# Reordering the projections of a retention head, and moving its value transposes, in a two-layer streaming trunk on one Trainium2 core

## The chip, the cores and the metric

The kernel runs on one core of a Trainium2 chip. The metric is the device time of one execution in microseconds (us), the median of three runs; one execution was profiled besides, and all rows below come from it.

## What is computed

Two layers over 528 tokens (16 learned ones ahead of 512) and 1024 channels. Each layer normalises its input, projects it into 14 x 1024 channels, runs a short convolution branch and a retention branch with four heads, gates both, projects the sum and adds it to the residual:

```python
for l in range(DEPTH):
    xn = _rmsnorm(h, pre_norm_g[l])
    proj = xn @ w_in[l] + b_in[l]
    c_h, c_b, c_c, c_z, r_q, r_k, r_v, r_z, g_a, g_b = jnp.split(proj, split_at, axis=-1)
    y_a = _short_conv_branch(c_h, c_b, c_c, c_z, conv_w[l], conv_b[l], w_conv_out[l])
    y_b = _retention_branch(r_q, r_k, r_v, r_z, ret_gn_g[l], w_ret_out[l])
    y = jax.nn.sigmoid(g_a) * y_a + jax.nn.sigmoid(g_b) * y_b
    h = h + _rmsnorm(y @ w_o[l], post_norm_g[l])
```

In the retention branch a head has 256 query and key channels, 512 value channels and 512 gate channels. Queries and keys are rotated by position, scores of query and key are weighted with a decay and multiplied with the values; the result is normalised per head and token, multiplied with silu of the gate channels, and projected back with w_ret_out.

## The kernel before, in words

Channels lie on the partitions and tokens along the free axis. All products are made with fp32r operands in two parts (hi and lo), three matmuls for one: hi x hi, hi x lo, lo x hi. ScalarE makes the hi part (a cast, L142) and VectorE the lo part (a subtraction, L143), for weights as for activations.

The projections run in `Group`s (L284): one group makes 256 output channels for all tokens, by a block scheme with seven products (`mul`, L275) of 12 matmuls each. Six of them run in the group itself; the seventh, with the call that hands over the result (`end`, L358), runs behind the first two products of the next job (`close`). Each product is evicted by ScalarE (`put`, L322, rows of L325, and L335) into SBUF; a group uses two PSUM tiles `pb` and `pc` and the shared `pa`. `RetOut` (L521) multiplies a quarter of the previous head's finished output with w_ret_out: two results of 24 matmuls each (L244) into a two-bank PSUM tile `pp`, of which there are two; VectorE adds the result to YB (L540), for head 0 ScalarE copies it (L538).

Between these jobs stands the work on whole heads. It is put into the stream by `later(delay, fn)` (L127): after `delay` more ticks, and a tick is one product of a group, or half of one result of `RetOut`: 12 matmuls in both cases (6 where 512 tokens go in one piece). What is called there for a head:

- `rope` (L395): the rotation of keys or queries, two steps of three VectorE operations (L403 to L405) and a split each; called when the group of the keys or queries ends (`k_done`, `q_done`).
- `scores` (L412), 8, 10 and 12 ticks behind the end of the queries.
- `vtrans` (L441): PE transposes values by token block (L447) into `pp`; per block ScalarE evicts twice (L454 with a read of its accumulator, L455; once L459) and VectorE once (L460). Called 3, 6 and 9 ticks behind the end of the second group of values (`v_done`, L844), where also two sets of tiles are taken and ScalarE copies the last 64 tokens twice (`twice`).
- behind the end of the second group of gates (`z_done`, L855): `attend` (L463) at 1, 3, 5 and 7 ticks, each with evictions L492, L493 and the sum of squares L496; the sum over partitions and its power (`rstd_token`, L366: PE L370, VectorE L374, GpSimd L375) at 10; its spreading over the partitions (`spread`, L378: PE L384, ScalarE L387) at 13; and the normalisation of the four result tiles (`finish`: VectorE L514, then a split) at 14 to 17. These four tiles are what `RetOut` of this head reads, in the stream of the next head.

For heads 1 to 3 the order of jobs is keys, queries, first values, two `RetOut`, second values, two `RetOut`, gates, gates (L883 and below); head 3's `RetOut`s stand among groups of the convolution branch. Head 0 has another order, written out at the start of each layer, and its own delays (16 or 12 ticks for the transposes).

The framework records these calls in program order and then orders the instructions of each engine by priority and by when its own model holds an operand for ready; so instructions of neighbouring jobs change places. Every engine then runs its list strictly in that order. Tiles of SBUF with the tag `r` come from one pool of 26.

Of the kernel before, what the change touches and what calls it, by code (L numbers as in the profile page):

```python
# [25 lines left out]
DK = 256  # L26
DV = 512
# [6 lines left out]
R_Q = 4 * D  # L34
R_K = R_Q + H * DK
R_V = R_K + H * DK
# [20 lines left out]
def trunk(ctx: ExitStack, tc: tile.TileContext, xT, w_in, binT, w_co, w_ro, w_o, gpre, gpost,  # L57
# [19 lines left out]
    def rslot(w=T):  # L77
        return gr.tile([P, w], F32R, tag="r", name=nm("r"))

    def fslot(w=T, dt=F32):  # L80
        return gr.tile([P, w], dt, tag="r", name=nm("f"))
# [45 lines left out]
    def later(delay, fn):  # L127
        now[1] += 1
        heappush(queue, (now[0] + delay, now[1], fn))
# [260 lines left out]
    def twice(dst, src):  # L390

        nc.scalar.copy(dst.rearrange("p (a b) -> p a b", a=2),
                       src[:, T - CHUNK:T].unsqueeze(1).to_broadcast([P, 2, CHUNK]))
# [47 lines left out]
    def vtrans(vt, v8, V, js):  # L441

        pp = pslot()
        for b, j in enumerate(js):
            k0, kn, _ = JT[j]
            for v in range(4):
                nc.tensor.transpose(pp[0:kn, b, v * P:(v + 1) * P], vt[v][:, k0:k0 + kn] if j < 4 else v8[:, v, :], ident)  # L447
        for b, j in enumerate(js):
            kn = JT[j][1]
            pv = pp[0:kn, b, :]  # L450
            s = sm.tile([P, 1], F32, tag="vs", name=nm("vs"))[0:kn]
            hi, lo = V[j]
            with tc.high_priority():
                nc.scalar.activation(hi[0:kn], pv, AF.Copy, scale=-1.0 / DV, accum_out=s)  # L454
                nc.scalar.activation(hi[0:kn], pv, AF.Identity, bias=s)  # L455
                r0 = 0
                if j == len(JT) - 1:
                    r0 = CHUNK
                    nc.scalar.activation(lo[0:r0], pv[0:r0], AF.Identity, bias=s[0:r0])  # L459
                nc.vector.scalar_tensor_tensor(lo[r0:kn], pv[r0:kn], s[r0:kn], hi[r0:kn].bitcast(F32),  # L460
                                               op0=ALU.add, op1=ALU.subtract)
# [334 lines left out]
    for l in range(DEPTH):  # L796
# [7 lines left out]
        hd = heads(0)  # L804
# [12 lines left out]
        def add(job, *args, todo=todo):  # L817
            todo.append((job, args))
            return job

        def k_done(ts, hd):
            a, b, hd["k"] = rope(ts, 0)

            def k8():
                hd["k8"] = rslot(512).rearrange("p (n c) -> p n c", n=4)
                for n in range(4):
                    twice(hd["k8"][:, n, :], hd["k"][n // 2][n % 2].bitcast(F32))
            later(0, a)
            later(2, b)
            later(3, k8)  # L830
# [13 lines left out]
        def v_done(ts, hd, d=3):  # L844
            hd["vt"] = hd.get("vt", []) + list(ts)
            if len(hd["vt"]) == 4:
                vt = hd["vt"]
                v8 = fslot(512).rearrange("p (v c) -> p v c", v=4)
                for v in range(4):
                    twice(v8[:, v, :], vt[v])  # L850
                hd["V"] = V = [(rslot(512), rslot(512)) for _ in JT]
                for n, js in enumerate(((0, 1), (2, 3), (4,))):
                    later(d + 3 * n, lambda js=js: vtrans(vt, v8, V, js))

        def z_done(ts, hd, h, l, yr, silu=(1,)):  # L855
            cs = slice(QCOLS[l].t0, T)
            for n in silu:
                nc.scalar.activation(ts[n][:, cs], ts[n][:, cs], AF.Silu)
            hd["zt"] = hd.get("zt", []) + list(ts)
            if len(hd["zt"]) < 4:  # L860
                return

            def start():
                hd["sums"] = fslot()
                hd["n"] = normed(l, hd["zt"], hd["sums"], yr)
            later(0, start)
            for v in range(4):
                later(1 + 2 * v, lambda v=v: attend(l, h, *hd["S"], hd["V"], v, hd["zt"][v], hd["sums"]))
            later(10, lambda: hd["n"][0]())
            later(13, lambda: hd["n"][1]())  # L870
            for v in range(4):
                later(14 + v, lambda v=v: hd["n"][2](v))

        hd["done"] = (k_done, q_done, v_done, z_done)
        yrs = jb["yrs"] = [[] for _ in range(H)]
# [6 lines left out]
        add_conv(0)  # L882
        for h in range(1, H):  # L883
            d = {}
            add(Group(l, R_K + h * DK, I_ALL[l], lambda ts, d=d: k_done(ts, d)))
            add(Group(l, R_Q + h * DK, I_Q[l], lambda ts, d=d, h=h, l=l: q_done(ts, d, h, l)))
            add(Group(l, R_V + h * DV, I_ALL[l], lambda ts, d=d: v_done(ts, d)))
            for q in (0, 1):
                add(RetOut(l, h - 1, q), yrs[h - 1])
            add(Group(l, R_V + h * DV + 256, I_ALL[l], lambda ts, d=d: v_done(ts, d)))  # L890
            for q in (2, 3):
                add(RetOut(l, h - 1, q), yrs[h - 1])
            for b in range(2):
                add(Group(l, R_Z + h * DV + b * 256, I_Q[l],
                          lambda ts, d=d, h=h, l=l, yr=yrs[h]: z_done(ts, d, h, l, yr), AF.Silu))
# [364 lines left out]
```

## Time and profile before

| | us |
|---|---|
| median of 3 runs | 1603.13 |
| lowest and highest run | 1600.23, 1605.2 |
| the profiled execution | 1600.25 |
| its span, first to last instruction | 1598.4 |
| PE (matmul) busy | 1553.9 |
| VectorE (DVE) busy | 1168.9 |
| ScalarE (ACT) busy | 910.2 |

How to read it: PE matmuls overlap, so their busy time is longer than the distance between their starts; a wait is idle time of an engine just ahead of an instruction, put down to what came last. Times in a row count from the span's start. A window row gives the PE's granted clock as a share of full speed (2.4 GHz): 1.00 is that level, 0.50 the other, 1.2 GHz.

### The profile page before, as it was taken

The page shows a single profiled execution, that of the slowest core. Times are in us where ns is not written, and L with a number is a line of the kernel's source. Part 1 is how long each engine was busy: PE and PEld are TensorE (multiplying, and loading weights), DVE is VectorE, ACT ScalarE, POOL GpSimd, SP SyncE. Part 2 cuts the span into 40 slices and gives each one's busy share as a digit, 9 for nine tenths or more (in the row PEclk, how much of TensorE's full clock was granted, in tenths as well). Part 3 has the DMA queues.
Part 4 walks back from the last instruction along what each step waited for, and adds up shares of the span by engine and source line. Part 5 has one row for each costly group of instructions (what it writes and reads, how often), then busy time and mean ns, then how long its engine had stood idle before and what let it go on. Part 6 is the DMA issues. An engine that isn't in the chain of part 4 may idle for free.

```text
span 1598.4 us, 29227 instructions
## 1 busy us (share of the span) xinstructions
PE 1553.9 (97%) x11762; PEld 1494.1 (93%) x11762; DVE 1168.9 (73%) x1702; ACT 910.2 (57%) x1763; POOL 28.9 (2%) x23
## 2 busy tenths in 40 slices
PE   9999999899999999999999999999999999999998
PEld 9989999898999999999999998998998999999986
DVE  6996966776776788866376889678777777997542
ACT  6675565464565466655345666655654655676531
POOL 0000000001000000000000000000000000000000
PEclk9999999999999999999999999999999999999999
DMA  7132332232222243335321223222322223334421
GB/s 263 67 113 73 106 107 89 83 108 97 89 103 87 91 141 128 133 123 180 119 101 53 100 94 113 103 103 95 111 93 80 101 98 119 132 126 145 142 98 53
DMA packets 86039, 174.37 MB, mean 109 GB/s; under 512 B 11280, under 2 KB 15888, under 8 KB 85904
## 3 DMA queue, kind: packets, MB, share of 16 engines
q1 hardware_dynamic: 85760, 172.50, 31.2%
q8 instruction: 92, 1.51, 0.4%
q14 instruction: 43, 0.35, 0.1%
q10 hardware_dynamic: 144, 0.01, 0.0%
HBM read 168.21 MB, written 4.26 MB: 108 GB/s over the span
## 4 chain that ended last, share of the span: by engine, by line
PE 79%; DVE 10%; ACT 5%; issue 3%; DMA 3%; POOL 1%; SPq 0%; DVEq 0%; POOLq 0%; ACTq 0%
PE pb L279 25%; PE pp L244 15%; PE pc L279 13%; PE pp L648 7%; PE pa L279 6%; PE pp L481 4%; PE pp L1122 3%; PE pb L648 3%; DVE wlo L143 2%; PE pp L422 2%; DMA raw<-in_w_in 2%; ACT whi L142 2%; DVE r L143 1%; PE pp L384 1%; PE pp L447 1%
## 5 line engine op out<-in xcount | busy, mean ns | idle before, releaser
L143 DVE TENSOR_TENSOR wlo<-raw,whi 128x1024 fp32r<-128x1024 f32 (+2 forms) x358 | 392.7, 1107 | 120.4 <-ACT whi L142 117.5
L142 ACT CAST whi<-raw 128x1024 fp32r<-128x1024 f32 (+2 forms) x358 | 339.4, 959 | 227.8 <-PE pp L244 63.7
L279 PE MATMUL pb<-Xh,whi 128*128 128x264 f32 (+2 forms) x1008 | 287.7, 285 | 2.2 <-ACT pa L335 1.2
L279 PE MATMUL pb<-Xl,whi 128*128 128x264 f32 (+2 forms) x1008 | 285.0, 283 | 0.0
L279 PE MATMUL pb<-Xh,wlo 128*128 128x264 f32 (+2 forms) x1008 | 284.7, 283 | 0.1
L244 PE MATMUL pp<-r,whi 128*128 128x264 f32 (+1 forms) x1152 | 251.2, 325 | 5.6 <-ACT r L142 4.8
L279 PE MATMUL pc<-Xh,whi 128*128 128x264 f32 (+2 forms) x672 | 194.4, 289 | 8.1 <-ACT f L325 7.8
L244 PEld LDWEIGHTS pp<-r,whi 128*128 128x128 f32 x1152 | 176.3, 188 | 23.7 <-ACT r L142 5.9
L279 PEld LDWEIGHTS pb<-Xh,whi 128*128 128x128 f32 x1008 | 189.6, 188 | 4.4 <-ACT pa L335 1.6
L279 PE MATMUL pc<-Xl,whi 128*128 128x264 f32 (+2 forms) x672 | 192.0, 286 | 0.0
L279 PE MATMUL pc<-Xh,wlo 128*128 128x264 f32 (+2 forms) x672 | 191.5, 285 | 0.0
L279 PEld LDWEIGHTS pb<-Xl,whi 128*128 128x128 f32 x1008 | 189.6, 188 | 0.6
L279 PEld LDWEIGHTS pb<-Xh,wlo 128*128 128x128 f32 x1008 | 189.3, 188 | 0.5 <-DVE wlo L143 0.3
L244 PE MATMUL pp<-r,wlo 128*128 128x264 f32 (+1 forms) x576 | 153.1, 321 | 1.4 <-DVE wlo L143 1.4
L307 DVE TENSOR_TENSOR raw<-raw 128x512 f32<-128x512 f32 x168 | 115.1, 686 | 41.4 <-DMA raw<-in_w_in 40.9
L279 PEld LDWEIGHTS pc<-Xh,whi 128*128 128x128 f32 x672 | 128.0, 190 | 12.3 <-ACT f L325 11.2
L279 PEld LDWEIGHTS pc<-Xl,whi 128*128 128x128 f32 x672 | 127.9, 190 | 0.4
L279 PEld LDWEIGHTS pc<-Xh,wlo 128*128 128x128 f32 x672 | 127.8, 190 | 0.3
L244 PEld LDWEIGHTS pp<-r,wlo 128*128 128x128 f32 x576 | 95.3, 188 | 9.8 <-DVE wlo L143 2.0
L279 PE MATMUL pb<-Xh,whd 128*128 128x264 f32 (+2 forms) x336 | 96.7, 288 | 1.1 <-ACT f L325 1.1
L279 PE MATMUL pa<-Xh,whi 128*128 128x264 f32 (+2 forms) x336 | 96.7, 288 | 0.0
L279 PE MATMUL pa<-Xl,whi 128*128 128x264 f32 (+2 forms) x336 | 95.7, 285 | 0.0
(219 smaller groups left out, 3300.3 us busy)
## 6 DMA issues: line engine op xcount, KB each, us to landing
raw<-in_w_in SPq DMA_DIRECT2D x426, 256.0 KB, 2.9
raw<-in_w_ro SPq DMA_DIRECT2D x32, 512.0 KB, 3.2
raw<-in_w_in SPq DMA_DIRECT2D x20, 512.0 KB, 4.8
raw<-in_w_co SPq DMA_DIRECT2D x16, 512.0 KB, 3.2
raw<-in_w_o SPq DMA_DIRECT2D x16, 512.0 KB, 3.9
Dsb<-in_decay SPq DMA_DIRECT2D x8, 520.0 KB, 3.9
h1d<-f SPq DMA_DIRECT2D x8, 264.0 KB, 4.5
f<-h1d SPq DMA_DIRECT2D x8, 264.0 KB, 4.3
```

The source lines that it names most:

```text
L142: nc.scalar.copy(dst_hi, src)
L143: nc.vector.tensor_tensor(dst_lo, src, dst_hi.bitcast(F32), op=ALU.subtract)
L244: nc.tensor.matmul(banks[i][:, 0:cols.n], wt(k)[:, msl], xs(k)[:, sl], start=(k == 0 and a == 0), stop=(k == nk - 1 and a == 2),)
L279: nc.tensor.matmul(o[:, 0:n], wt[:, k, :], xs[:, blk, k, HALF - n:], start=(first and k == 0 and a == 0), stop=(k == 3 and a == 2), skip_g ...
L307: nc.vector.tensor_tensor(r[:, 512:], r[:, 512:], r[:, 0:512], op=ALU.add)
L384: nc.tensor.matmul(pp[:, c // per, (c % per) * sc:(c % per + 1) * sc], y[:, c:c + 1].to_broadcast([sc, P]), ident[0:sc, 0:sc], start=True, ...
L422: nc.tensor.matmul(pp[0:kn, n + i, 0:cols.n], k[dt][x][:, k0:k0 + kn] if j < 4 else k8[:, dt * 2 + x, :], q[dt][y][:, sl], start=(dt == 0 ...
L447: nc.tensor.transpose(pp[0:kn, b, v * P:(v + 1) * P], vt[v][:, k0:k0 + kn] if j < 4 else v8[:, v, :], ident)
L481: nc.tensor.matmul(pp[:, b, lo_ - banks[b][0]:hi_ - banks[b][0]], V[j][x][0:kn, v * P:(v + 1) * P], S[0:kn, SOFF[j] + lo_ - q0:SOFF[j] + h ...
L648: nc.tensor.matmul(o, wt(k), xs[:, i0:], start=(k == 0 and a == 0), stop=(k == KD - 1 and a == 2))
L1122: nc.tensor.matmul(o, x[:, xs], wo[k][half][w], start=(k == 0 and a == 0), stop=(k == KD - 1 and a == 2))
```

## The change

Four edits. The order of jobs for heads 1 to 3 becomes first values, second values, keys, two `RetOut`, queries, two `RetOut`, gates, gates. The values are transposed 34, 37 and 40 ticks behind the end of the second group of values, where they were at 3, 6 and 9. The tiles for the copies of the last tokens and those for the transposed values are taken 32 and 34 ticks behind it (for head 0 at 14 and 16, or 10 and 12), and no longer at once. The spreading and the normalisation come one tick later, at 14 and at 15 to 18.

```diff
@@ v_done
-                v8 = fslot(512).rearrange("p (v c) -> p v c", v=4)
-                for v in range(4):
-                    twice(v8[:, v, :], vt[v])
-                hd["V"] = V = [(rslot(512), rslot(512)) for _ in JT]
+                hd["V"] = V = []
+
+                def places():
+                    V.extend((rslot(512), rslot(512)) for _ in JT)
+
+                def v8():
+                    hd["v8"] = fslot(512).rearrange("p (v c) -> p v c", v=4)
+                    for v in range(4):
+                        twice(hd["v8"][:, v, :], vt[v])
+
+                later(d - 2, v8)
+                later(d, places)
                 for n, js in enumerate(((0, 1), (2, 3), (4,))):
-                    later(d + 3 * n, lambda js=js: vtrans(vt, v8, V, js))
+                    later(d + 3 * n, lambda js=js: vtrans(vt, hd["v8"], V, js))
@@ z_done
             later(10, lambda: hd["n"][0]())
-            later(13, lambda: hd["n"][1]())
+            later(14, lambda: hd["n"][1]())
             for v in range(4):
-                later(14 + v, lambda v=v: hd["n"][2](v))
+                later(15 + v, lambda v=v: hd["n"][2](v))
@@ for h in range(1, H)
             d = {}
+            for n in range(2):
+                add(Group(l, R_V + h * DV + n * 256, I_ALL[l], lambda ts, d=d: v_done(ts, d, 34)))
             add(Group(l, R_K + h * DK, I_ALL[l], lambda ts, d=d: k_done(ts, d)))
-            add(Group(l, R_Q + h * DK, I_Q[l], lambda ts, d=d, h=h, l=l: q_done(ts, d, h, l)))
-            add(Group(l, R_V + h * DV, I_ALL[l], lambda ts, d=d: v_done(ts, d)))
             for q in (0, 1):
                 add(RetOut(l, h - 1, q), yrs[h - 1])
-            add(Group(l, R_V + h * DV + 256, I_ALL[l], lambda ts, d=d: v_done(ts, d)))
+            add(Group(l, R_Q + h * DK, I_Q[l], lambda ts, d=d, h=h, l=l: q_done(ts, d, h, l)))
             for q in (2, 3):
                 add(RetOut(l, h - 1, q), yrs[h - 1])
```

What it does to the order of instructions, at three places. In all of them head 1 of layer 0 is the head whose output is normalised or, in the third, head 2 the one whose values are transposed; the other heads read alike.

VectorE, from the mean of squares (L374, for the power L375) to the first normalising product (L514), before:

```order
L374 TENSOR_SCALAR nv_3442<-pp_3435 88x6
L143 TENSOR_TENSOR r_3387<-f_3381,r_3386 128x528
L403 TENSOR_TENSOR f_3403<-f_3080,sin_sb 128x528
L404 TENSOR_TENSOR f_3404<-f_3081,cos_sb 128x528
L143 TENSOR_TENSOR wlo_3466<-raw_3118,whi_3465 128x1024
L405 TENSOR_TENSOR f_3403<-f_3403,f_3404 128x528
L143 TENSOR_TENSOR r_3409<-f_3403,r_3408 128x528
L356 TENSOR_TENSOR f_3260<-f_3260,f_3261 128x528
L514 TENSOR_TENSOR f_2830<-f_2830,f_3502 128x528
```

and now:

```order
L374 TENSOR_SCALAR nv_3424<-pp_3417 88x6
L143 TENSOR_TENSOR wlo_3443<-raw_3118,whi_3442 128x1024
L356 TENSOR_TENSOR f_3260<-f_3260,f_3261 128x528
L143 TENSOR_TENSOR wlo_3481<-raw_3120,whi_3480 128x1024
L143 TENSOR_TENSOR wld_3696<-t_3587,whd_3695 128x512
L514 TENSOR_TENSOR f_2739<-f_2739,f_3499 128x528
```

The rotation of the keys (L403 to L405 and the two subtractions into `r`) is gone from this place; it now stands beside the first two `RetOut`, the rotation of the queries beside the last two. On PE 48 matmuls of groups now lie between L370 and L384 in every head, where it was 24 for heads 1 and 2 and 36 for heads 0 and 3; between L384 and the first matmul of `RetOut` it is 48 for heads 1 and 2, where it was 72.

ScalarE, around the copy of the spread factors (L387), which needs PE's L384, before:

```order
L335 ACTIVATE pa_108<-pb_3475,bin_92 128x264
L387 COPY f_3502<-pp_3503 128x528
L392 CAST r_3446<-r_3387 128x128
L392 CAST r_3446<-r_3408 128x128
L392 CAST r_3446<-r_3409 128x128
L325 ACTIVATE f_3474<-pc_3476 128x264
```

and now:

```order
L325 ACTIVATE f_3451<-pc_3453 128x264
L142 CAST whd_3695<-t_3587 128x512
L325 ACTIVATE f_3259<-pb_3262,bin_92 128x264
L387 COPY f_3499<-pp_3500 128x528
L142 CAST r_3522<-f_2739 128x528
L325 ACTIVATE f_3451<-pb_3452 128x264
```

The eviction of `pc` by L325 stood behind the copy and stands ahead of it now; the casts for the rotated keys are gone.

ScalarE, the last two of the five value blocks of head 2 (L454, L455, L459) and the evictions behind them, before:

```order
L454 ACTIVATE r_3970,vs_4092<-pp_4079 128x512
L142 CAST whi_4125<-raw_3730 128x1024
L455 ACTIVATE r_3970<-pp_4079,vs_4092 128x512
L142 CAST whi_4173<-raw_3835 128x1024
L454 ACTIVATE r_3972,vs_4151<-pp_4146 128x512
L455 ACTIVATE r_3972<-pp_4146,vs_4151 128x512
L459 ACTIVATE r_3973<-pp_4146,vs_4151 64x512
L325 ACTIVATE f_4131<-pc_4133 128x264
```

and now:

```order
L454 ACTIVATE r_4196,vs_4293<-pp_4280 128x512
L142 CAST whi_4325<-raw_3956 128x1024
L455 ACTIVATE r_4196<-pp_4280,vs_4293 128x512
L325 ACTIVATE f_4225<-pa_108 128x264
L454 ACTIVATE r_4198,vs_4353<-pp_4348 128x512
L142 CAST whi_4374<-raw_4097 128x1024
L455 ACTIVATE r_4198<-pp_4348,vs_4353 128x512
L459 ACTIVATE r_4199<-pp_4348,vs_4353 64x512
L325 ACTIVATE f_4226<-pc_4229,bin_92 128x264
```

Before, PE ran `RetOut` at this time, whose results VectorE takes for heads 1 and 2; now it runs the two groups of gates, whose products ScalarE evicts.

## Rows read from the trace of the kernel before

**Rows 1.** The page's first part: busy time, share of the span, instructions.

```profile
PE 1553.9 (97%) x11762; PEld 1494.1 (93%) x11762; DVE 1168.9 (73%) x1702; ACT 910.2 (57%) x1763; POOL 28.9 (2%) x23
```

**Rows 2.** Waits of PE, whole span: who waited for whom, total us, times, longest.

```profile
PE pc L279 <- ACT f L325: 7.8, 9, 1.6
PE pp L384 <- POOL ny L375: 6.5, 4, 3.0
PE pp L244 <- ACT r L142: 4.8, 4, 1.3
PE pp L370 <- DVE f L496: 4.2, 3, 3.3
```

**Rows 3.** Timeline of PE: start, length, what, count, idle before and its releaser.

```profile
141.34 0.87 PE L370 MATMUL pp<-ones_d,f 128*88 128x1 f32 x5 [3.33 <-DVE f L496]
275.98 1.07 PE L370 MATMUL pp<-ones_d,f 128*88 128x1 f32 x12 [0.35 <-DVE f L496]
283.11 1.57 PE L384 MATMUL pp<-ident,ny 88*128 88x88 f32 x12 [3.01 <-POOL ny L375]
290.46 0.29 PE L279 MATMUL pa<-Xh,whi 128*128 128x264 f32 x1
294.84 0.40 PE L244 MATMUL pp<-r,whi 128*128 128x264 f32 x2
301.95 0.51 PE L244 MATMUL pp<-r,whi 128*128 128x264 f32 x2 [1.12 <-ACT r L142]
508.59 1.47 PE L384 MATMUL pp<-ident,ny 88*128 88x88 f32 x12
1080.30 0.39 PE L279 MATMUL pc<-Xh,whi 128*128 128x264 f32 x1 [1.60 <-ACT f L325]
```

**Rows 4.** Windows, PE: stretch, length, busy (count), granted clock, DMA share, GB/s.

```profile
143.10:145.90 2.80, 2.80 (x14) 0.50 0.27 94
...
284.50:287.10 2.60, 2.60 (x15) 0.53 0.00 0
287.10:289.00 1.90, 1.90 (x13) 0.74 0.00 0
396.60:398.70 2.10, 2.05 (x13) 0.67 0.38 152
398.70:401.10 2.40, 2.40 (x14) 0.58 0.00 0
1077.00:1083.00 6.00, 4.19 (x33) 1.00 0.29 105
```

**Rows 5.** Timeline of GpSimd: the power, for heads 1 and 3 of layer 0.

```profile
278.34 4.71 POOL L375 TENSOR_TENSOR ny<-nv,mhalf 88x6 f32<-88x6 f32 x1 [132.93 <-DVE nv L374]
...
504.63 1.32 POOL L375 TENSOR_TENSOR ny<-nv,mhalf 88x6 f32<-88x6 f32 x1 [108.03 <-DVE nv L374]
```

**Rows 6.** Timelines of VectorE and ScalarE ahead of the wait at 301.95.

```profile
299.66 0.70 DVE L405 TENSOR_TENSOR f<-f,f 128x528 f32<-128x528 f32 x1
300.45 0.63 ACT L142 CAST r<-f 128x528 fp32r<-128x528 f32 x1 [3.95 <-DVE f L405]
301.27 0.62 ACT L142 CAST r<-f 128x528 fp32r<-128x528 f32 x1
```

**Rows 7.** Timeline of ScalarE: head 3's last cast of the same kind.

```profile
520.73 0.63 ACT L142 CAST r<-f 128x528 fp32r<-128x528 f32 x1
```

**Rows 8.** Groups by line, ScalarE: busy us, mean ns | idle before, releasers.

```profile
L455 ACT ACTIVATE r<-pp,vs 128x512 fp32r<-128x512 f32 (+1 forms) x40 | 27.6, 691 | 0.9
L454 ACT ACTIVATE r<-pp 128x512 fp32r<-128x512 f32 (+1 forms) x40 | 23.9, 598 | 31.3 <-PE pp L447 25.0 <-DVE r L460 6.3
```

**Rows 9.** Waits of PE in 95 to 130 us: head 0 of layer 0.

```profile
PE pc L279 <- ACT f L325: 2.1, 2, 1.2
```

**Rows 10.** The same view, 900 to 930 us: head 0 of layer 1.

```profile
PE pc L279 <- ACT f L325: 1.2, 1, 1.2
```

**Rows 11.** Timeline of VectorE ahead of the wait at 141.34.

```profile
138.49 0.69 DVE L307 TENSOR_TENSOR raw<-raw 128x512 f32<-128x512 f32 x1 [1.60 <-DMA raw<-in_w_in]
```

## The prediction

> **What bounds the kernel now.** I read the page's shares first: PE is busy for 97% of the span, VectorE for 73% and ScalarE for 57% [rows 1]. So the kernel is bound by PE, the change neither adds nor removes a matmul, and what can be won is what PE loses between matmuls. The list of PE's waits comes next [rows 2]; it names who ends them. Then I look at where the large ones lie [rows 3]: at 283 us and, by the same count, in three more places, PE waits for GpSimd's power ahead of L384; some 19 us later it waits for a cast of ScalarE ahead of `RetOut`'s L244; in layer 1 it also waits for an eviction of `pc`. These places are the handovers of heads 1 and 2 in both layers, four in all. Last I read the granted clock behind the long waits [rows 4]: behind a wait of 3.0 us it falls to the 1.2 GHz level for a while, behind one of 1.6 us in layer 1 it stays at 2.4.
>
> The unit for what follows: from 290.46 to 294.84 PE issues 36 matmuls of 264 columns without a wait [rows 3], 0.122 us each. 12 of them, a tick, are 1.46 us.
>
> **What goes.** Four terms.
>
> 1. *The wait for the power.* From L370 at 275.98 to L384 at 283.11 are 7.1 us [rows 3], of which 24 matmuls fill 2.9 and the power alone takes 4.71 [rows 5]. Now 48 matmuls stand there: L370's 1.0 and 5.9 make 6.9 us. With a power as slow as that, 0.2 us of waiting would be left. But for head 3, where VectorE has no rotation in this place, the same power took 1.32 [rows 5], and the change takes the rotation away for heads 1 and 2 too. I count all 6.5 us of it [rows 2].
> 2. *The clock behind it.* Two of these waits were long enough to lower the clock. Window by window, length times the share not granted: 2.6 x 0.47 + 1.9 x 0.26 = 1.7 us for head 1, 2.1 x 0.33 + 2.4 x 0.42 = 1.7 us for head 2 [rows 4]. Together 3.4.
> 3. *The wait ahead of `RetOut`.* PE waits at 301.95 for the cast that makes the hi part of the fourth normalised tile [rows 3]. ScalarE makes that cast at 301.27, behind one at 300.45 for which it had sat idle for 3.95 us, for L405 of the rotation of the queries [rows 6]. With both rotations behind the first `RetOut` this order can't arise. All four waits of this kind go: 4.8 us [rows 2].
> 4. *Two small ones.* In layer 1 the eviction of `pc` no longer stands behind L387 (second order above): two waits of 1.6 us [rows 3] of the 7.8 in the list, 3.2. Ahead of L370 PE waits for the sum of squares, 4.2 us in all, of which 3.33 belong to head 0 [rows 2, 3]; in the other two places VectorE had two operations of the rotation ahead of it. 0.9.
>
> Sum: 6.5 + 3.4 + 4.8 + 3.2 + 0.9 = 18.8 us.
>
> A rule bears on the second term. The rows say that two of two waits of 3.0 us lowered the clock, and the sum counts both. The Trainium skill ("TensorE: Matmul & The Clock Gate", Part 1) says that the gate watches activity in stretches that run on by themselves, so that the same kernel shows different numbers of slow matmuls from run to run. By that rule other executions of the kernel before may lose less there, and the sum would be 15.4; no row here shows a 3 us wait without the fall.
>
> **What is added or moved.**
>
> - *The transposes among the gates.* Now each of the five value blocks is evicted by ScalarE while it also evicts the groups' products. Bounds: nothing, as between the `RetOut`s now; or what head 0 pays, whose transposes already stand among groups at the same distance of three ticks: 2.1 us in layer 0 [rows 9] and 1.2 in layer 1 [rows 10], for three heads each, 9.9 us. Which end is nearer? Between the last transpose and the product that needs `pc` again PE has 29 matmuls, 3.5 us. In that time ScalarE has L454 (0.60), L455 and L459 (0.69 each) [rows 8], and a weight cast of 1024 columns, by the 0.63 for 528 columns [rows 6] an estimated 1.2, and then the eviction: 3.2 and the eviction, about even. So a wait, but a short one: I take 0.6 per head, 3.6 us.
> - *Both rotations among the `RetOut`s.* One rotation is eight operations of VectorE of 0.70 [rows 6], 5.6 us, beside two `RetOut` of 48 matmuls (11.7 us) and their four additions. VectorE is then nearly full, and the scores behind the last `RetOut` may find the second part of the queries late. Nothing, or what such a late operand costs now ahead of `RetOut`, 4.8 / 4 = 1.2 us, for six heads 7.2. The order holds 8 matmuls of a group in front of the last four of the first scores, 1.0 us of cover, so nearer to nothing: 0.3 each, 1.8 us.
> - *Less room ahead of `RetOut`.* 48 matmuls behind L384 where it was 72. PE reads the fourth tile after 9 matmuls of `RetOut`, 12 of the group's last product and 9 more: 78 in all, 9.5 us behind L384. Head 3, which has no rotation in the way, begins that cast at 520.73, 10.7 us behind the end of its L384 (508.59 + 1.47) [rows 3, 7], so the tile is there after 11.3; but VectorE has six operations of the convolution in between, some 4.2 us at 0.70 each [rows 6]. For heads 1 and 2 I take 11.3 - 4.2 = 7.1: in time. Head 3 itself loses 12 to 20 matmuls of its room; 0 to 2 us each, I take 0.5, 1.0 us.
> - *Tiles and DMA.* Weight loads keep their sizes and places: the jobs are still three groups, two `RetOut`, a group, two `RetOut`, two groups. The decay tables are loaded a group later, behind scores that are long done. The values' tiles are held for 32 more ticks, but the ten tiles for the transposed values are taken that much later. Nothing; the cover is that each weight is split about one job ahead.
>
> Sum: 3.6 + 1.8 + 1.0 = 6.4 us. Net: 18.8 - 6.4 = 12.4 us less than the profiled execution's 1600.25: 1587.9. That execution lies 2.9 us under the median of the runs, 1603.13; from the median it is 1590.7. I say 1590.
>
> **The rivals.**
>
> *Everything goes and nothing comes.* The transposes are covered and the clock counts in full: 1603.1 - 18.8 = 1584.3. If head 0's stall at 141.34, 3.33 us with the clock at 0.50 behind it [rows 3, 4], should happen to dissolve, since VectorE's list at the start also changes a little, 4.7 more: 1579.6. For it: the stall hangs on a weight DMA for which VectorE waited 1.60 us [rows 11]. Against: the loads are the same. Chance 0.15.
>
> *The clock was not really there* (the rule above): 15.4 - 6.4 = 9.0, 1594. Chance 0.15.
>
> *The waits only change place.* The transposes cost as much as head 0's, 9.9, and the fourth tile takes head 3's whole 11.3 us for heads 1 and 2 also, a wait of 1.8 at four places, 7.2: 18.8 - 17.1 = 1.7 us gained, 1601. For it: head 0 is the only row of transposes among groups. Against: head 0's evictions stand behind more of them in ScalarE's list. Chance 0.1.
>
> *Slower: ScalarE's list is held up by VectorE among the gates.* An L454 waits for an L460 of an earlier block; ScalarE now loses 6.3 us in all that way [rows 8], where it evicts nothing that PE needs soon. If VectorE, ahead of that L460, waits for a weight DMA as at 138.49 [rows 11], the eviction of `pc` behind L454 comes late, PE stops for some 3 us and the clock falls: 3.0 + 1.7 = 4.7 us a head, 28.2 for six, 1612.5. It decides from 18.8 / 6 = 3.1 us a head. For it: VectorE does wait for weights. Against: head 0 met the same with 1.2 us at most at once [rows 9], and its clock did not fall for it. Chance 0.07.
>
> That the change does nothing to the order is excluded by the three places shown.
>
> **How the numbers follow.** My forecast, a gain of 9 to 16 us, has 0.53, and the rivals 0.15, 0.15, 0.1 and 0.07. The measurement can tell about 0.3%, 4.8 us, from no change, so slower begins at 1608 and faster below 1598.3. Faster: 0.53 + 0.15 + 0.15, 0.83; within 0.3%: 0.10; slower: 0.07. The range leaves out the slower rival and the lower half of the first: 1579 to 1601.
>
> **What would show it.** Right: no wait at L384 for the power over 0.5 us and no clock under 0.9 in these two places; the power of heads 1 and 2 under 2.5 us; no wait of L244 for a cast; the waits of `pc` for L325 now at the gates, under 1 us each. Wrong: a wait of 3 us anywhere in heads 1 to 3, a new fall of the clock, waits of L422 for casts of the queries over 1 us each, or a stall of L244 for VectorE's additions.

## The result, and the profile after

The changed kernel takes 1585.55 us, the median of four runs (1584.71 to 1592.18), beside 1603.67 for the kernel before: a ratio (of the means of the runs) of 0.9899, 95% interval 0.9868 to 0.993. In a second comparison it was 0.9903 (0.9884 to 0.9921). The forecast was 1590, its range 1579 to 1601. The profiled execution took 1584.71 us where that of before took 1600.25, 15.5 less; its span is 1582.9. The page's first part, to be held against [rows 1]:

```profile
PE 1545.6 (98%) x11762; PEld 1491.0 (94%) x11762; DVE 1169.5 (74%) x1702; ACT 909.7 (57%) x1763; POOL 18.8 (1%) x23
```

VectorE and ScalarE do the same work as before. GpSimd is busy 10.1 us less, and PE 8.3 us less for the same 11762 matmuls. Where that lies, windows of PE show: each stretch runs from the L370 of one head to that of the next (heads 0, 1, 2 of layer 0, then of layer 1). Columns: stretch, length, PE busy (instructions), granted clock, DMA share, GB/s. Before:

```profile
141.34:275.98 134.64, 133.59 (x1048) 0.97 0.30 102
275.98:389.53 113.55, 108.66 (x857) 0.98 0.27 94
389.53:503.25 113.72, 109.00 (x856) 0.98 0.27 94
945.61:1073.41 127.80, 126.49 (x917) 1.00 0.31 108
1073.41:1180.74 107.33, 103.88 (x725) 1.00 0.28 99
1180.74:1287.92 107.18, 103.88 (x724) 1.00 0.27 94
sum 704.22, PE 685.49; mean PE 114.25
```

and now:

```profile
141.99:280.00 138.01, 134.32 (x1048) 0.97 0.29 100
280.00:389.94 109.94, 107.09 (x856) 1.00 0.28 97
389.94:497.95 108.01, 106.31 (x857) 1.00 0.28 98
940.34:1067.39 127.05, 125.62 (x917) 1.00 0.31 109
1067.39:1170.93 103.54, 102.42 (x724) 1.00 0.29 102
1170.93:1273.63 102.70, 101.82 (x724) 1.00 0.28 98
sum 689.25, PE 677.57; mean PE 112.93
```

These six stretches hold 704.22 - 689.25 = 15.0 of the 15.5 us. The four handovers of heads 1 and 2 give 3.6 to 5.7 each; the first stretch, where head 1's values are now transposed among its gates, has become 3.4 longer. Idle time (length less busy) falls from 18.7 to 11.7, and busy time by 7.9.

PE's waits over the whole span, to be held against [rows 2], and GpSimd's power for head 1, against [rows 5]:

```profile
PE pc L279 <- ACT f L325: 12.2, 13, 1.6
PE pp L370 <- DVE f L496: 4.8, 3, 3.6
PE pp L481 <- DVE r L460: 1.6, 3, 0.7
```

```profile
281.42 1.32 POOL L375 TENSOR_TENSOR ny<-nv,mhalf 88x6 f32<-88x6 f32 x1 [135.36 <-DVE nv L374]
```

The waits of L384 for the power (6.5) and of L244 for a cast (4.8) are gone; the power fell from 4.71 to 1.32. What is new stands at the gates, where the values are transposed. The timeline of PE in head 1 of layer 0, the worst place, and a window of PE behind it:

```profile
241.81 0.39 PE L279 MATMUL pc<-Xh,whi 128*128 128x264 f32 x1 [0.58 <-ACT f L325]
247.57 0.49 PE L481 MATMUL pp<-Shi,r 80*128 80x208 f32 x2 [0.66 <-DVE r L460]
249.44 0.40 PE L279 MATMUL pc<-Xh,whi 128*128 128x264 f32 x1 [1.02 <-ACT f L325]
```

```profile
250.10:253.60 3.50, 3.50 (x18) 0.51 0.49 154
```

Three waits within 9 us, none over 1.02, and the clock falls to the 1.2 GHz level for 3.5 us: a new fall, 3.5 x 0.49 = 1.7 us. Head 0, too, now waits longer for `pc`: of the 12.2 us 5.9 are its own, where it was 3.7 of the 7.8 in [rows 2].

### The profile page after: what moved, and what is told of

The parts are those of the page before. It is cut to its first block, busy times and chain, and to the rows that moved or that the text cites. A ratio compares the mean times of both kernels' runs of the same rounds, so it can differ in the third digit from the quotient of the medians.

```text
span 1582.9 us, 29259 instructions
## 1 busy us (share of the span) xinstructions
PE 1545.6 (98%) x11762; PEld 1491.0 (94%) x11762; DVE 1169.5 (74%) x1702; ACT 909.7 (57%) x1763; POOL 18.8 (1%) x23
## 4 chain that ended last, share of the span: by engine, by line
PE 81%; DVE 7%; ACT 6%; issue 3%; DMA 3%; SPq 0%; DVEq 0%; POOLq 0%; ACTq 0%
PE pb L279 26%; PE pp L244 16%; PE pc L279 13%; PE pp L648 7%; PE pa L279 7%; PE pp L481 4%; PE pp L1130 3%; PE pb L648 3%; DMA raw<-in_w_in 2%; DVE wlo L143 2%; ACT whi L142 2%; PE pp L422 2%; PE pp L384 1%; ACT r L454 1%; ACT r L455 1%
## 5 line engine op out<-in xcount | busy, mean ns | idle before, releaser
L143 DVE TENSOR_TENSOR wlo<-raw,whi 128x1024 fp32r<-128x1024 f32 (+2 forms) x358 | 392.9, 1107 | 140.7 <-ACT whi L142 138.3
L244 PE MATMUL pp<-r,whi 128*128 128x264 f32 (+1 forms) x1152 | 245.9, 321 | 0.0
L279 PE MATMUL pc<-Xh,whi 128*128 128x264 f32 (+2 forms) x672 | 193.7, 288 | 12.3 <-ACT f L325 12.2
L244 PEld LDWEIGHTS pp<-r,whi 128*128 128x128 f32 x1152 | 177.5, 188 | 15.9 <-ACT whi L142 0.5
L244 PE MATMUL pp<-r,wlo 128*128 128x264 f32 (+1 forms) x576 | 152.8, 321 | 0.0
L244 PEld LDWEIGHTS pp<-r,wlo 128*128 128x128 f32 x576 | 95.5, 188 | 8.0
L314 DVE TENSOR_TENSOR raw<-raw,raw 128x512 f32<-128x512 f32 x84 | 57.9, 689 | 51.8 <-DMA raw<-in_w_in 51.3
```

The source lines that it names most:

```text
L143: nc.vector.tensor_tensor(dst_lo, src, dst_hi.bitcast(F32), op=ALU.subtract)
L244: nc.tensor.matmul(banks[i][:, 0:cols.n], wt(k)[:, msl], xs(k)[:, sl], start=(k == 0 and a == 0), stop=(k == nk - 1 and a == 2),)
L279: nc.tensor.matmul(o[:, 0:n], wt[:, k, :], xs[:, blk, k, HALF - n:], start=(first and k == 0 and a == 0), stop=(k == 3 and a == 2), skip_g ...
L314: nc.vector.tensor_tensor(b[:, 0:512], a[:, 512:], c[:, 0:512], op=ALU.add)
```

## The experiments

Ratios are to the kernel before, run beside each, with 95% intervals. Three questions, in the order in which they came up, and a version that goes further.

**What took the waits away: the rotation's place or the later tick?** Of the four edits, the last was not run by itself in the new order. It does move instructions there: with the old delays (13, and 14 to 17) in the changed kernel, L384 of every head stands behind 36 matmuls of groups where the change has 48, and ScalarE has the eviction of `pc` by L325 behind L387 again. For the power neither 36 nor 48 is needed: in the change it ends 2.74 us behind the start of L370 (280.00; 281.42 + 1.32), and L370 with 24 matmuls takes 3.9. What the tick is worth otherwise in the new order is open. In the old order it costs:

```diff
# the kernel before
-            later(13, lambda: hd["n"][1]())
+            later(14, lambda: hd["n"][1]())
-                later(14 + v, lambda v=v: hd["n"][2](v))
+                later(15 + v, lambda v=v: hd["n"][2](v))
```

> The kernel before with only the fourth edit: spreading and normalisation one tick later, the old order of jobs. Theory 1 (the rotation next to the power is the cause, the tick only adds matmuls): the power of heads 1 and 2 still takes 4.7 and 2.65 us; 36 matmuls stand between L370 and L384 where 24 stood, 1.46 us more, so the two waits of 3.0 at L384 fall to about 1.5, the two of 0.2 vanish, and the clock no longer falls behind them: 3.4 + 3.4 gained. The normalised tiles come a tick later and the four waits of L244 for the cast grow by up to 1.46 each, 0 to 5.8 lost. 1596 to 1602 where the kernel before has 1603. Rival (the tick is what removed the waits): no wait at L384 is left, the waits of L244 don't grow, and the gain is 9.9: 1593.

Measured: 1613.2 us, ratio 1.005 (1.0031 to 1.007): slower. PE's largest wait, and the clock behind a wait of 2.6 us:

```profile
PE pp L244 <- ACT r L142: 10.7, 4, 2.7
```

```profile
303.30:306.10 2.80, 2.78 (x12) 0.50 0.02 6
```

Neither theory had this. The scheduler left L384 of heads 1 and 2 where it was, behind 24 matmuls, so its waits stayed at the 6.5 us of [rows 2]. Only the normalisation came a tick later, and the four waits of L244 went from 1.2 to 2.7 each. The second run moved the rotation instead:

```diff
# the kernel before
-            add(Group(l, R_K + h * DK, I_ALL[l], lambda ts, d=d: k_done(ts, d)))
+            add(Group(l, R_K + h * DK, I_ALL[l], lambda ts, d=d: k_done(ts, d, 7)))
@@ k_done(ts, hd, late=0)
-            later(0, a)
-            later(2, b)
-            later(3, k8)
+            later(late, a)
+            later(late + 2, b)
+            later(late + 3, k8)
```

> The kernel before with only the rotation of the keys of heads 1 to 3 moved, 7 ticks later, so that on VectorE none of it stands between the mean of squares (L374) and the first normalising product (L514); order of jobs and delays as before. Theory 1: the power of heads 1 and 2 falls from 4.71 and 2.65 to 1.3 and 1.0, all four waits at L384 go (6.5) and both falls of the clock (3.4); the rotations now stand beside the normalisation, so the four waits of L244 stay or grow (1.2 each, to at most 2.5): 1594 to 1599. Rival (any work of VectorE stretches the power alike): the power stays over 2.5 us, the waits at L384 at 1 us or more, and the time at 1600 to 1603.

Measured: 1627.31 us, 1.0142 (1.0118 to 1.0165). GpSimd's power for head 1 and VectorE behind its L374 (with the idle time before), PE's largest wait, and one of these in the timeline of PE:

```profile
280.12 1.32 POOL L375 TENSOR_TENSOR ny<-nv,mhalf 88x6 f32<-88x6 f32 x1 [131.78 <-DVE nv L374]
282.33 1.23 DVE L143 TENSOR_TENSOR wlo<-raw,whi 128x1024 fp32r<-128x1024 f32 x1 [2.29 <-ACT whi L142]
```

```profile
PE pp L244 <- ACT r L142: 28.3, 8, 5.9
```

```profile
307.50 1.55 PE L244 MATMUL pp<-r,whi 128*128 128x264 f32 x5 [4.33 <-ACT r L142]
```

So what VectorE did beside the power is what stretched it: without that 1.32 us, and no wait at L384 is left, with the same order of jobs and the same tick (L384 of heads 1 and 2 now stands behind 36 matmuls of groups and not 24, but 24 would have covered this power too). Theory 1 names the rotation, its rival any work of VectorE, and this run can't part the two, for VectorE sat idle beside the power, for 2.29 us. Rows of other heads speak for the rival. In the kernel before, head 0's power (143.70) takes 1.71 us beside a single addition of weights (L315, 0.68). In the faster version at the end of this section it has a weight subtraction (L143, 1.23) and L356 (0.70) beside it, and no rotation:

```profile
145.81 2.27 POOL L375 TENSOR_TENSOR ny<-nv,mhalf 88x6 f32<-88x6 f32 x1 [111.15 <-DVE nv L374]
```

Beside the 4.71 us of [rows 5] there were six operations of VectorE, five of them of the rotation. So the rotation was the largest part of the cause, not the only kind of it.

The wait only moved, and grew: the rotation now stands ahead of the tiles that `RetOut` reads. At both places tried, beside the power and beside the normalisation, it costs; the new order of jobs takes it out of both at once, which neither run could.

**Why do the transposes cost among the gates?** First the suspicion that ScalarE is held up by the two buffers of the one-column sum `vs`, which two consecutive L454 share with their L460:

```diff
# the changed kernel
-            s = sm.tile([P, 1], F32, tag="vs", name=nm("vs"))[0:kn]
+            s = sm.tile([P, 1], F32, tag="vs", name=nm("vs"), bufs=10)[0:kn]
```

> The changed kernel with ten buffers instead of two for the one-column sums of the value blocks, so that an L454 need not wait for the L460 of two blocks earlier; the order on every engine is the same. Theory A (among the gates ScalarE's list is simply full, the evictions of pc stand behind casts and transposes): the idle time of L454 for L460, 5.0 us in all, goes, but most of it is at head 0; the waits of pc at the gates of heads 1 to 3 stay (7.9 us with those of L481, now at least 6), head 0's four of 0.2 to 1.6 shrink by up to 1.3 each: 0 to 4 us faster than the change. Theory B (ScalarE is held up by the two buffers): the waits at the gates go as a whole, and the fall of the clock behind them: 8 us or more faster than the change.

Measured: 1588.95 us, 0.9896 (0.9877 to 0.9916), the change's own ratio. But the edit did not take the wait away; ScalarE's list of waits still reads

```profile
ACT r L454 <- DVE r L460: 5.0, 6, 1.3
```

The buffers are not what ties an L454 to an L460, and the run says nothing for either theory. Then the distance between the transposes:

```diff
# the changed kernel
-                    later(d + 3 * n, lambda js=js: vtrans(vt, hd["v8"], V, js))
+                    later(d + (4 if d > 30 else 3) * n, lambda js=js: vtrans(vt, hd["v8"], V, js))
-                add(Group(l, R_V + h * DV + n * 256, I_ALL[l], lambda ts, d=d: v_done(ts, d, 34)))
+                add(Group(l, R_V + h * DV + n * 256, I_ALL[l], lambda ts, d=d: v_done(ts, d, 31)))
```

> The changed kernel with the three transposes of heads 1 to 3 at 31, 35 and 39 ticks behind the values instead of 34, 37 and 40. Theory A (ScalarE's list is too full where three transposes stand three ticks apart): a tick more between them, 1.46 us, is more than any of the waits; the waits of pc at the gates fall from 6.3 us to under 3, those of L481 for L460 (1.6 us, the last block is now a tick earlier) go, and so does the fall of the clock at 250 us (1.7): 4 to 7 us faster than the change. Rival (each pair of blocks by itself delays the eviction behind it): the waits stay within 2 us, and the time too.

Measured: 1577.04 us, 0.9831 (0.9805 to 0.9858), faster than both kernels and about 11 us faster than the change, where 4 to 7 were expected; the waits at the gates are nearly gone, and so is the fall of the clock there. This moves two things, distance and place, so the next run kept the distance (the second line of that diff alone: 31, 34, 37), beside the change itself:

> The changed kernel with the three transposes at 31, 34 and 37 ticks: three ticks earlier, but still three apart. Theory A (it is the crowding of ScalarE's list by transposes three ticks apart that counts): the waits of L481 for L460 go, since the last block is earlier, but the waits of pc stay, 0.6 to 1.1 us once or twice a head: 1 to 4 us faster than the change. Rival (it is the nearness of the last block to the products with the values): with the last block three ticks earlier all of it goes, as with 31, 35 and 39: 8 us or more faster than the change.

> The changed kernel once more, beside the three that follow. Both theories: the same waits to a tenth of a us (they come from the order), 0.987 to 0.993 of the kernel before. What may differ is the clock: if the fall at 250 us comes of the three waits of 0.58, 0.66 and 1.02 close together, it is there again, in the same place; if it is an accident of that execution, it is gone or elsewhere.

Measured: 1576.11 us, 0.9826 (0.9806 to 0.9847), for 31, 34, 37; 1588.55, 0.9903, for the change. The whole gain came without the wider distance, so theory A falls. The change repeated its waits of 0.65 and 1.02 in head 1, but that of 0.58 ahead of them did not come, and nor did the fall of the clock there. One as long came elsewhere, behind waits of 1.44 and 0.32 us (L648) that the first execution has as well, without a fall. Windows of PE some 1.4 us behind the second of them, in the first execution and in this one:

```profile
840.20:843.60 3.40, 3.40 (x31) 1.00 0.02 5
839.90:843.30 3.40, 3.40 (x18) 0.50 0.02 5
```

PE's list of waits for 31, 34, 37 begins

```profile
PE pc L279 <- ACT f L325: 5.9, 6, 1.5
```

and none of the six lies at the gates of heads 1 to 3. What is it then? ScalarE in the change, head 2 of layer 0, with PE's matmul that waits for the last row:

```profile
358.02 0.61 ACT L454 ACTIVATE r<-pp 128x512 fp32r<-128x512 f32 x1
...
358.59 1.06 ACT L142 CAST whi<-raw 128x1024 fp32r<-128x1024 f32 x1
359.53 0.71 ACT L455 ACTIVATE r<-pp,vs 128x512 fp32r<-128x512 f32 x1
360.11 0.68 ACT L459 ACTIVATE r<-pp,vs 64x512 fp32r<-64x512 f32 x1
360.68 0.48 ACT L325 ACTIVATE f<-pc,bin 128x264 f32<-128x264 f32 x1
```

```profile
361.21 0.39 PE L279 MATMUL pc<-Xh,whi 128*128 128x264 f32 x1 [1.01 <-ACT f L325]
```

A group fills `pc` twice. Between the first filling and the second PE has three products of other tiles, between the second and the next group's only two. The third call of the transposes brings the last of the five value blocks; call it the third block, as the expectations do. In the change it is transposed behind a second filling: ScalarE has all of it, and a cast, ahead of the eviction, and PE only 29 matmuls. With 31, 34, 37 it stands two products ahead of the second filling. Theory C: that place within the group decides, not earlier or later. The third block one tick later than in the change, then one earlier:

```diff
# the changed kernel, in one run 35, in the other 33
-                add(Group(l, R_V + h * DV + n * 256, I_ALL[l], lambda ts, d=d: v_done(ts, d, 34)))
+                add(Group(l, R_V + h * DV + n * 256, I_ALL[l], lambda ts, d=d: v_done(ts, d, 35)))
```

> The changed kernel with the transposes one tick later, at 35, 38 and 41. Theory C (what counts is where the third block falls among a group's products: in the change ScalarE has all of it, L454 to L459, ahead of the eviction of the pc that PE wants back after only 29 matmuls): now the order has that eviction ahead of the third block, so the waits of pc and of L481 at the gates of heads 1 to 3 go although the block is later: 8 to 10 us faster than the change, 1576 to 1580. Rival (the third block is too near to the products with the values, and 31 ticks helped by being earlier): the waits grow by up to 1.46 us each, and the time is 1588 or more.

> The changed kernel with the transposes one tick earlier, at 33, 36 and 39. Theory C: on ScalarE the third block now has the cast ahead of it and the pc's eviction behind it, but it stands ahead of the product that fills this pc, 12 matmuls earlier, and is done by the time that product ends: no wait of pc at the gates over 0.3 us, 1576 to 1580. Rival (nearness): one tick is a third of the way to 31, the waits lose up to 1.46 us each and some stay: 1581 to 1585.

Measured: 1576.89 us, 0.9817 (0.9799 to 0.9834), one tick later; 1587.92, 0.989 (0.9875 to 0.9904), one tick earlier. The later one is as theory C has it: ScalarE has the eviction ahead of the third block,

```profile
355.09 0.48 ACT L325 ACTIVATE f<-pc,bin 128x264 f32<-128x264 f32 x1
...
356.76 0.62 ACT L454 ACTIVATE r<-pp 128x512 fp32r<-128x512 f32 x1
```

and of the waits of `pc` one is left in heads 1 to 3 (1.62, in head 3, where ScalarE had sat idle for 2.43 us for VectorE's L356, which stood behind a weight load). So place, and not nearness, accounts for these waits. The earlier one lost its waits of `pc` at these gates, as expected, but not its time: the eviction of another tile, `pb`, now came late. PE's list, and parts of the timelines of VectorE, ScalarE and PE:

```profile
PE pb L279 <- ACT pa L335: 9.3, 8, 1.8
```

```profile
343.89 0.69 DVE L314 TENSOR_TENSOR raw<-raw,raw 128x512 f32<-128x512 f32 x1 [1.41 <-DMA raw<-in_w_in]
...
345.44 0.74 DVE L460 SCALAR_TENSOR_TENSOR r<-pp,vs,r 80x512 fp32r<-80x512 f32 x1
```

```profile
346.22 0.60 ACT L454 ACTIVATE r<-pp 128x512 fp32r<-128x512 f32 x1 [1.42 <-DVE r L460]
...
346.80 0.45 ACT L335 ACTIVATE pa<-pb,bin 128x264 f32<-128x264 f32 x1
```

```profile
347.30 0.39 PE L279 MATMUL pb<-Xh,whi 128*128 128x264 f32 x1 [1.15 <-ACT pa L335]
```

The rows fit the chain of the prediction's slower rival: VectorE stands at a weight load, its L460 behind it, an L454 waits for that, and the eviction that PE wants stands behind the L454. No run cut the chain, so it is read from the rows and not tested. The wait costs 1.0 to 1.8 us a head here. One more run tried to cut it at the buffers of `vs` (ten instead of two, on 33, 36, 39):

> The version with 33, 36 and 39 ticks, and ten buffers instead of two for the sums of the value blocks; the order on every engine is that of 33, 36, 39. Theory D (the waits of pb for L335 there, 8 us in six places, come of a chain: VectorE stands at a weight load with an L460 behind it, an L454 waits for that L460 because there are two buffers only, and ScalarE's L335 stands behind the L454): the idle time of L454 for L460, 13 us, goes, the waits of pb for L335 at the gates fall under 0.5 us each, and the time to that of 31 or 35 ticks: 1575 to 1580. Rival (ScalarE has too much work ahead of that L335, whatever the L460 does): the waits stay over 0.8 us each, the time within 3 us of 33, 36, 39 (1588, 0.989 of the kernel before).

Measured: 1587.51 us, 0.9891 (0.9868 to 0.9913); L454 still waits 12.7 us for L460, so the buffers are not the link, and the expectation's rival, 1588, came. In the program only the second block of each `pp` waits for VectorE, the first waits for PE; whether giving each block its own accumulator would cut the link wasn't tried.

**Could the transposes have stayed among the `RetOut`s?** At 23, 26 and 29 ticks they stand beside the last two:

> The changed kernel with the transposes at 23, 26 and 29 ticks, among the last two RetOut, where in the kernel before they stood too, and beside the rotation of the queries. Theory A (transposes cost what they do because ScalarE also evicts groups there): the waits of pc and of L481 at the gates go (7.9 us and the clock behind them, 1.7), and ScalarE is free where they now stand; but VectorE has there the rotation of the queries, the additions of RetOut and the L460, and the pool of 26 tiles holds RetOut's eight, so a wait of L422 for the queries or of L447 for an accumulator comes up: 0 to 2 us a head. 1574 to 1586. Rival (the pool or VectorE becomes the bound there): waits of 2 us or more a head, and slower than the change.

Measured: 1628.65 us, 1.0153 (1.0134 to 1.0171). The waits at the gates went but for one of 0.44, but `RetOut` and transposes now share the two accumulators `pp`, and VectorE reads the second block late:

```profile
PE pp L244 <- DVE r L460: 22.3, 6, 3.8
```

The rival of that expectation held. At these ticks, beside the rotation of the queries, the transposes can't stay among the `RetOut`s; other ticks there weren't tried.

**A version that beats both.** With 31, 35, 39, and for head 0 the transposes four ticks apart and the sum, spreading and normalisation three ticks later:

```diff
# on top of 31, 35, 39
-    v_done(vt, hd["hd"], 16)
+    v_done(vt, hd["hd"], 14)
-            v_done(opened[2:6], hd["hd"], 12)
+            v_done(opened[2:6], hd["hd"], 10)
-                    later(d + (4 if d > 30 else 3) * n, lambda js=js: vtrans(vt, hd["v8"], V, js))
+                    later(d + 4 * n, lambda js=js: vtrans(vt, hd["v8"], V, js))
+            late = 0 if h else 3
-            later(10, lambda: hd["n"][0]())
-            later(14, lambda: hd["n"][1]())
+            later(10 + late, lambda: hd["n"][0]())
+            later(14 + late, lambda: hd["n"][1]())
-                later(15 + v, lambda v=v: hd["n"][2](v))
+                later(15 + late + v, lambda v=v: hd["n"][2](v))
```

> The change with 31, 35 and 39 ticks, with head 0's transposes four ticks apart too (at 14, 18, 22 and 10, 14, 18), and for head 0 the sum over partitions three ticks later (13), spreading and normalisation at 17 and 18 to 21. Theory A: 36 matmuls, 4.4 us, now stand ahead of head 0's L370, which waited 3.6 us for a sum held up behind a weight load: that wait goes and the clock behind it stays up (2.3), and of head 0's waits of pc (1.8 in layer 0, 2.0 in layer 1) half goes: 6 to 8 us faster than 31, 35, 39 alone, 1568 to 1572. Rival (the kernel is short of weights there, and the wait only moves to the next weight): the waits of PE at 130 to 160 us stay at 3 us, and the time at 1575 to 1578.

Measured: 1568.42 us, 0.978 (0.976 to 0.9799). Head 0's L370, which waited 3.33 us in [rows 3], waits no more, though three others came up there (1.78 for an L460 at 117 us, 1.23 and 1.55 for `pc` at 141 and 160):

```profile
144.51 1.03 PE L370 MATMUL pp<-ones_d,f 128*88 128x1 f32 x12
```

A last shift for head 0 (13, 16, 19, in layer 1 9, 12, 15, and 31, 34, 37 for the others) brought nothing more:

> The version with head 0's sum three ticks later, with transposes at 31, 34 and 37 for heads 1 to 3 and at 13, 16, 19 (layer 1: 9, 12, 15) for head 0, so that there too no eviction of pc stands behind the third block within a group's shorter half. Theory C: the wait of 1.8 us of L481 for L460 at 117 us goes; two waits of pc at 141 and 160 us (1.2 and 1.5, not of the transposes) stay: 1565 to 1568. Rival (nearness and spacing count): no change against 14, 18, 22, 1568.

Measured: 1570.44 us, 0.9781 (0.9767 to 0.9796): the wait at 117 us went as theory C had it, but waits of `pb` for L335 (0.70, at 101 us) and of `pc` (1.35, at 901 us) stand in its place, and the time is that of the rival.

## Why the prediction was right

Sign and range held, and so did the main mechanism, that the power of heads 1 and 2 becomes short and PE no longer waits for it. How near the number came is in part luck, as the sums below show. Step by step:

- *The wait for the power*, 6.5: all gone. That VectorE's work beside it caused it is shown by the run that moved the rotation alone; rows of other heads say that it need not be the rotation. The other half of that step, that 48 matmuls would cover even a slow power, was not needed.
- *The clock behind it*, 3.4: gone, both stretches now at 1.00 where they stood at 0.98. For these falls the Trainium skill's rule ("TensorE: Matmul & The Clock Gate", Part 1), that the same kernel shows other numbers of slow matmuls from run to run, gave no discount, and the rival at 1594 built on it did not come. With shorter waits the traces agree with the rule: behind the same 1.44 and 0.32 us the changed kernel has 3.4 us at 0.50 in one execution and none in the other. The new fall at 250 us is no such case, since the execution without it also lacked the wait of 0.58.
- *The wait ahead of `RetOut`*, 4.8: gone, and no other wait of L244 took its place.
- *The two small ones*: the two waits of 1.6 for `pc` are gone, 3.2, but the working gave them the wrong cause. ScalarE in the kernel before, around the first of them:

```profile
1078.77 0.63 ACT L142 CAST r<-f 128x528 fp32r<-128x528 f32 x1 [1.91 <-DVE f L405]
...
1079.77 0.48 ACT L325 ACTIVATE f<-pc,bin 128x256 f32<-128x256 f32 x1
...
1080.86 0.61 ACT L387 COPY f<-pp 128x512 f32<-128x512 f32 x1
```

  PE went on at 1080.30 [rows 3], ahead of L387 and right behind the eviction of 1079.77; what had held that up is a cast of the rotation, for which ScalarE sat idle for 1.91 us. So these waits, too, came of the rotation, and they are missing from the run that moved it alone. The 0.9 ahead of L370 had the wrong sign: heads 1 and 2 of layer 0 now wait 0.68 and 0.43 there, 1.1.
- *The transposes among the gates*, forecast 3.6, is the term that was mis-sized. Measured for heads 1 to 3: seven waits of `pc`, 6.3 (0.58, 1.02, 1.01, 1.02 in layer 0, 0.70, 1.07, 0.88 in layer 1), and three of L481, 1.6; 7.9 in all, near the upper bound of 9.9, and the fall of the clock, 1.7, on top. The working had the right place (29 matmuls ahead of the eviction, ScalarE's list about as long) and called it even; it left out that ScalarE came into this stretch late already, with the fourth block's rows and another cast. A new fall of the clock was one of its signs of being wrong, and "under 1 us each" one of its signs of being right: the first came, the second failed for four of the seven.
- *Both rotations among the `RetOut`s*, forecast 1.8: 0.8, two waits of L422 of 0.19 and 0.63 in one head. *Less room ahead of `RetOut`*, forecast 1.0: nothing.
- *Head 0* had no term. Its waits of `pc` grew by 2.2 us; the change takes its tiles and copies later too, but what made them grow isn't known.

Gone: 6.5 + 3.4 + 4.8 + 3.2 = 17.9. Come: 7.9 + 1.7 + 0.8, and 0.2 at L370, 10.6. That leaves 7.3, and 15.5 were measured. Over the whole span PE is idle for 1598.4 - 1553.9 = 44.5 us before and for 37.3 now, 7.2 less, of which these terms hold 5.6; the other 1.6 are waits elsewhere that came and went, head 0's among them. And PE is busy for 8.3 us less, of which the clock is 1.7. The other 6.6 are a term that the sum did not have: time that PE loses and that counts as busy.

A part of it stands at the waits, which cost PE more than their idle time. In layer 1, where the clock stood at 1.00 in both kernels, the stretch of head 1 lost 3.45 - 1.12 = 2.3 us of idle time but also 103.88 - 102.42 = 1.5 of busy time, that of head 2 2.4 and 2.1. The timeline of PE around two waits of the kernel before:

```profile
1077.05 0.28 PE L279 MATMUL pb<-Xh,wlo 128*128 128x264 f32 x1
1077.54 1.16 PE L384 MATMUL pp<-ident,ny 128*128 128x128 f32 x8 [0.21 <-POOL ny L375]
...
1080.52 0.29 PE L279 MATMUL pc<-Xl,whi 128*128 128x264 f32 x1
```

Matmuls last 0.28 and start 0.12 apart. From 1077.05 to 1077.54 are 0.49 us, 0.37 more than from start to start without a wait, of which the list counts 0.21 as idle: 0.16 more. Behind the wait that ended at 1080.30 [rows 3] the next matmul starts after 0.22, 0.10 more. That is some 0.26 us a wait beside the idle time. Each of these two stretches had four such waits and has one now: 0.8 of the 1.5 and of the 2.1.

Over the whole span that is little, 1.3 us, for PE's list has 37 waits before and 32 now. A larger part stands among the matmuls of `RetOut`, in short pauses that no list of waits shows. Two L244 of 512 columns take 0.46 us from start to start (1101.89 to 1102.35 in the change); in the kernel before there are places like this, with 0.54:

```profile
1110.43 0.70 PE L244 MATMUL pp<-r,whi 128*128 128x512 f32 x2
1110.97 0.39 PE L244 MATMUL pp<-r,wlo 128*128 128x512 f32 x1
```

In the trace of before 53 starts beside an L244 come over 0.06 us late without a wait, 5.0 us together, in that of the change 16, 1.7 us: 3.4 of the 6.6, about half. What holds PE there the traces don't say, and no run tested it.

So the forecast came out near through errors that stood against each other: the transposes cost 4.3 more than it said, with the clock 6.0, and PE won 6.6 us of busy time for which it had no term. By the medians the gain is 18.1 us, by the means of the runs 16.2, between the profiled executions 15.5; the forecast had named 9 to 16. The number lies nearest to the rival at 1584.3, whose condition, that nothing comes, did not hold.

## What to carry to other kernels

A small operation that is slowed by another engine's work beside it has to be given a place without such work, and whatever is moved must not come to stand ahead of the next operand that PE needs: the rotation moved alone cost 23 us, moved with the jobs around it the same step paid. Before placing evictions of another kind into a stream of groups, read which PSUM tile PE wants back soonest and what stands ahead of its eviction in the evicting engine's list; three ticks earlier was worth 12 us here, one tick later as much, one tick earlier nothing. Read the distances between the starts of matmuls, and not the list of waits alone: of PE's gain here 6.6 us, 1.7 of the clock apart, stood in busy time.

## What the runs showed of the hardware that was not expected

- GpSimd's power on 88x6 elements took 1.32 us while VectorE sat idle, 1.71 beside one operation of VectorE (0.68), 2.27 beside two (1.23 and 0.70), and 4.71 beside the rotation with a weight subtraction; on 128x4 elements 2.65 beside the rotation and 1.02 without it.
- The clock stood at the 1.2 GHz level at or soon behind every wait of PE of 2.6 us and over in these traces, and behind shorter ones only sometimes. One wait of 1.71 us, of the same L648 for a cast of `Xh` between the layers, was followed by the low level in 7 of the 14 executions and not in the other 7.
- It also fell behind three waits close together of which none was over 1.02 (0.58, 0.66, 1.02; and 0.80, 0.67, 1.02 in the run with ten buffers on the change). Behind two of them (0.65 and 1.02), in the one execution that had just these, it stayed at 1.00:

```profile
250.50:253.00 2.50, 2.50 (x21) 1.00 0.67 207
```
